# First FF1 unit with plain block products for half of the tokens, output weights parted anew, end reordered

## The chip, the cores and the metric

The kernel runs on one core of one Trainium2 chip. The metric is device time in microseconds of one execution, as the median of several runs.

## The reference

One step of a small decoder trunk over 1024 prompt tokens and 64 sample tokens (8 sequences of 8), model width 1024, all in float32:

```python
h = rmsnorm(x, g1)
z = h @ w_in                                   # 1024 x 2816, split among three mixers
ya = gelu(za_u) * spatial(layernorm(gelu(za_v)))      # A: gMLP in chunks of 128 tokens
yb = silu(layernorm(conv31(zb_a * sigmoid(zb_g))))    # B: Conformer convolution
yc = zc_b * conv3(zc_c * zc_x)                        # C: short gated convolution
x = x + concat(ya, yb, yc) @ w_out             # 1024 x 1024
x = x + square(relu(rmsnorm(x, g2) @ w_ff1)) @ w_ff2  # 1024 x 4096, 4096 x 1024
y = rmsnorm(x, gf)
```

Beside y the kernel returns the convolutions' new states and the normalised v rows.

## The kernel before

Activations are kept transposed: features on the partitions, the 1088 tokens along the free axis. Every float32 operand is parted into a high and a low part of type float32r, and a product is made of three matmuls, high x high, high x low, low x high (`mm3`, lines 170 to 176). A weight's parting takes ScalarE one copy for the high part and VectorE one subtraction for the low part (`split`, L167 and L168), or, in the input projection, ScalarE the negative of the raw weight and GpSimd a transfer that adds the weight from DRAM to it (`split_far`, L482 and L483). Weights come raw, 512 KB each, on SP's queue (`load`, L161).

The stages follow one another: the mixers' input projection (weights 0 to 17), the output projection (weights 18 to 25, one for each block `fo` of 128 output features), 16 units of FF1 and 16 of FF2, and the last RMSNorm. From the output projection on, the tokens stand in two groups, A and B, of 544 each, a group in two halves of 272.

*Output projection.* Group A goes first, while the last mixer outputs are made. Three weights are begun with `out_first` (six of eight K tiles) and ended later, five follow in `out_job`; one weight's two parts lie in `wo2`, the others in a ring of two buffers per part (`hi`, `lo`). `in_job` calls `ahead_of` at its third column block, so that weight 19 is parted by `split_far` before weight 18 is used. `out_keep` (L921) stores the parts of weights `fo` 0 to 5 to DRAM (`wod`), and `out_fetch` (L926) reads them back for group B, whose jobs run in the order 6, 7, 0, 1, 2, 3, 4, 5, each followed by one entry of the list `rest` and three of the list `todo`, which holds group A's operands for FF1. Each job ends with `out_evac`: VectorE adds PSUM to the residual (L823), ScalarE squares it (L825), VectorE sums the squares (L829).

*FF1.* A unit is a 256 x 1024 slice of w_ff1, taken as a 2 x 2 block product with the Strassen-Winograd scheme: seven products (`s` = 0 to 6) of weight sums (`w_sums`, `w_parts`, L941 to L952) with sums of the normalised tokens (`x_norm` L878, `x_hi` L884, `x_lo` L888, `x_comb` L891). `steps` (L1260) lists all products; unit 0 takes group A's seven and then group B's seven, each step 12 matmuls of 272 columns, since group B's operands are made meanwhile by the entries of `x_ops(1)`; the units 1 to 29 take both groups in one step. Unit 0's results are copied from PSUM by ScalarE (L1113) and combined, squared and split later, from the list `later`, at fixed steps of unit 0 and 1 (L1114 to L1143); the parts go to DRAM for FF2 (`gr`, `gd`). Unit 1's weights were made early and stored to DRAM (`w1d`); each is loaded when unit 0 has used that slot for the last time (L1284).

*FF2 and the end.* FF2 uses the same scheme over pairs of units; each product of a step is added by VectorE to the accumulators (`ff2_out`, L1257). The two last units, 30 and 31, take group A through both units and then group B. `beside` holds what is issued with a step, between its matmuls and its evictions: loads, weight preparation (`prep`), the split of FF2's operands (`g_split`, L1216 and L1217), and for the last norm `fin_sqs`: squares on ScalarE (L1315), their sum on VectorE (L1317), the scaling by the norm's weight on ScalarE (L1321). Group A's outputs are scaled by GpSimd during group B's steps (`fin_out`, L1329). After the last step the squares of the last two accumulators' second halves are summed by VectorE, TensorE sums over the partitions, a Newton step on VectorE (`rstd_newton`, L134 to L139) gives the factor, and VectorE scales the eight blocks of group B, each stored by SP's or ScalarE's queue.

## Time and profile before

| | |
|---|---|
| median of 3 runs | 1120.68 us (1118.84 to 1123.88) |
| the profiled execution | 1121.21 us |
| its span | 1119.5 us |
| TensorE busy | 1048.1 us (94%) |
| VectorE busy | 879.0 us (79%) |
| ScalarE busy | 418.4 us (37%) |
| mean granted TensorE clock | 0.971 |

TensorE's busy time hardly leaves room, so the profile is read by stage: where a stretch is longer than TensorE's busy time in it, or where the granted clock is under 1.00. The stages in the trace: input projection 93 to 254 us, output projection to 373.8, FF1 unit 0 to 412.3, unit 1 to 437.3, then about 21.5 us a unit, the last two units 1040.4 to 1100.3, and the rest to 1119.5.

### The profile page before, as it was taken

The numbers are of one execution on the slowest core, as the hardware profiler recorded it, in microseconds if no ns is written. First come the engines' busy times: TensorE is split into PE (matmuls) and PEld (weight loads), VectorE is DVE, ScalarE is ACT, GpSimd is POOL, SyncE is SP. The second block draws the span as 40 slices with busy tenths as digits, with TensorE's granted clock in tenths as the row PEclk, the third lists the DMA queues.
The fourth block names the chain that finished last, engine by engine and source line by source line (L and its number), as shares of the span: only waits on it lengthen the run. The fifth ranks groups of instructions, "written<-read, shape, count | busy, mean of one in ns | idle before, by whom it ended". The sixth has DMA issues, their size and how long they took to land.

```text
span 1119.5 us, 19297 instructions
## 1 busy us (share of the span) xinstructions
PE 1048.1 (94%) x7524; PEld 1021.6 (91%) x7524; DVE 879.0 (79%) x1352; ACT 418.4 (37%) x711; POOL 123.5 (11%) x161
## 2 busy tenths in 40 slices
PE   8999999997899789999999999989999999999783
PEld 6789999996889679999999999989999999999773
DVE  6886999964468788778778878886788888888775
ACT  5533455323333333434434344344322222223332
POOL 3751524212000000000000000000000000000030
PEclk8999999998999999999999999999999999999896
DMA  6213454357897355546645645698866766655012
GB/s 222 99 41 73 102 93 80 77 109 209 275 324 238 113 168 184 204 158 215 217 159 194 219 169 181 213 394 289 247 208 216 238 187 227 217 181 194 1 60 101
DMA packets 94219, 198.61 MB, mean 177 GB/s; under 512 B 18288, under 2 KB 24432, under 8 KB 94128
## 3 DMA queue, kind: packets, MB, share of 16 engines
q1 hardware_dynamic: 90240, 183.95, 48.2%
q0 software_dynamic: 3312, 12.32, 6.8%
q8 instruction: 59, 0.97, 0.4%
q10 hardware_dynamic: 576, 1.11, 0.3%
q14 instruction: 32, 0.26, 0.1%
HBM read 129.03 MB, written 68.32 MB: 176 GB/s over the span
## 4 chain that ended last, share of the span: by engine, by line
DVE 38%; PE 35%; DMA 9%; issue 8%; ACT 8%; POOL 1%; SPq 1%; ACTq 0%; DVEq 0%; POOLq 0%
PE pp L174 11%; PE pp L176 11%; PE pp L175 11%; DVE gbuf L571 3%; DVE acc L571 3%; DMA wlo<-in_w 2%; ACT wsh L951 2%; DMA gr<-x_cn 2%; DVE x_cn L1119 1%; DMA gr<-x_cm 1%; DVE x_cn L1118 1%; DVE x_cn L1127 1%; DVE x_cm L1119 1%; DVE x_cm L1118 1%; DVE x_cm L1127 1%
## 5 line engine op out<-in xcount | busy, mean ns | idle before, releaser
L176 PE MATMUL mm<-xh,wlo 128*128 128x384 f32 (+1 forms) x336 | 109.8, 327 | 1.0 <-DMA wlo<-in_w 1.0
L174 PE MATMUL mm<-xh,whi 128*128 128x384 f32 (+1 forms) x336 | 110.2, 328 | 0.0
L175 PE MATMUL mm<-xl,whi 128*128 128x384 f32 (+1 forms) x336 | 109.5, 326 | 0.0
L174 PE MATMUL pp<-xah,wsh 128*128 128x272 f32 x256 | 76.2, 298 | 5.5 <-ACT x_cm L1113 5.0
L176 PE MATMUL pp<-xah,wsh 128*128 128x272 f32 x256 | 74.5, 291 | 0.0
L175 PE MATMUL pp<-xal,wsh 128*128 128x272 f32 x256 | 74.3, 290 | 0.0
L1257 DVE TENSOR_TENSOR x_cn<-pp,x_cn 128x544 f32<-128x544 f32 (+1 forms) x100 | 61.9, 649 | 10.6 <-PE pp L176 10.5
L176 PEld LDWEIGHTS mm<-xh,wlo 128*128 128x128 f32 x336 | 63.1, 188 | 1.6 <-DMA wlo<-in_w 1.6
L174 PE MATMUL pp<-xah,wsl 128*128 128x272 f32 x208 | 61.2, 294 | 2.6 <-ACT x_cm L1113 1.8
L174 PEld LDWEIGHTS mm<-xh,whi 128*128 128x128 f32 x336 | 63.1, 188 | 0.3
L175 PEld LDWEIGHTS mm<-xl,whi 128*128 128x128 f32 x336 | 63.1, 188 | 0.3
L176 PE MATMUL pp<-xah,wsl 128*128 128x272 f32 x208 | 61.1, 294 | 0.0
L175 PE MATMUL pp<-xal,wsl 128*128 128x272 f32 x208 | 60.9, 293 | 0.0
L1257 DVE TENSOR_TENSOR acc_al<-pp,acc_al 128x544 f32<-128x544 f32 (+1 forms) x68 | 44.3, 652 | 20.1 <-PE pp L176 20.0
L1302 POOL DMA_DIRECT2D acc_ah<-x2d x2 | 1.8, 906 | 504.3 <-DMA xbl<-gd 484.1
L174 PEld LDWEIGHTS pp<-xah,wsh 128*128 128x128 f32 x256 | 48.6, 190 | 9.1 <-ACT x_cm L1113 7.1
L951 ACT ACTIVATE wsh<-x_cm 128x512 fp32r<-128x512 f32 x29 | 18.3, 632 | 82.7 <-DVE x_cm L942 82.6
L175 PEld LDWEIGHTS pp<-xal,wsh 128*128 128x128 f32 x256 | 48.8, 191 | 0.0
L176 PEld LDWEIGHTS pp<-xah,wsh 128*128 128x128 f32 x256 | 48.7, 190 | 0.0
L1257 DVE TENSOR_TENSOR acc_ah<-pp,acc_ah 128x544 f32<-128x544 f32 (+1 forms) x68 | 44.2, 650 | 2.7 <-PE pp L176 2.5
L174 PEld LDWEIGHTS pp<-xah,wsl 128*128 128x128 f32 x208 | 40.1, 193 | 3.1 <-ACT x_cm L1113 2.0
L174 PE MATMUL pp<-xbh,wsl 128*128 128x272 f32 x144 | 41.9, 291 | 0.0
(510 smaller groups left out, 3884.4 us busy)
## 6 DMA issues: line engine op xcount, KB each, us to landing
gr<-x_cn SPq DMA_DIRECT2D x64, 272.0 KB, 4.0
wraw<-in_w SPq DMA_DIRECT2D x32, 512.0 KB, 5.0
gr<-x_cm SPq DMA_DIRECT2D x56, 272.0 KB, 5.5
raw<-in_w SPq DMA_DIRECT2D x25, 512.0 KB, 6.8
wlo<-in_w POOLq DMA_DIRECT2D x15, 512.0 KB, 7.4
wrawoh<-in_w SPq DMA_DIRECT2D x15, 512.0 KB, 4.4
wrawol<-in_w SPq DMA_DIRECT2D x15, 512.0 KB, 5.8
xah<-gr SPq DMA_DIRECT2D x26, 272.0 KB, 5.6
```

The costliest lines, as they stand in the source:

```text
L174: pe.matmul(ps, ah, bh, start=first, stop=False, skip_group_check=chain)
L175: pe.matmul(ps, ah, bl, start=False, stop=False, skip_group_check=chain)
L176: pe.matmul(ps, al, bh, start=False, stop=last, skip_group_check=chain)
L571: dve.scalar_tensor_tensor(out=d, in0=src, scalar=w, in1=d, op0=ALU.mult, op1=ALU.add)
L951: act.activation(out=hi, in_=src, func=AF.Copy)
L1118: dve.tensor_tensor(out=c, in0=c if u == 0 else ps, in1=slot(add, last)[1], op=ALU.add)
L1119: dve.scalar_tensor_tensor(out=c, in0=c, scalar=0.0, in1=c, op0=ALU.max, op1=ALU.mult)
L1127: dve.tensor_tensor(out=c.bitcast(F32R), in0=c, in1=slot(name + "h", True)[1], op=ALU.subtract)
L1257: dve.tensor_tensor(out=a, in0=ps, in1=a, op=ALU.add)
L1302: at(first_use[u + 2 * i, 0] + 1, lambda fo=fos[i]: gp.dma_start(out=acc(fo), in_=x2d[fo], accum_op=ALU.add))
```

## The change

1. `in_job` no longer calls `ahead_of` for job 18, so weight 19 is parted by `split` with VectorE, when the first output job is issued, and weight 21's load comes later on SP's queue.
2. `wod`, `out_keep` and `out_fetch` go. Only the weights 6 and 7 are kept for group B; the others are loaded raw again (`out_load`) and parted anew with an accumulating transfer (`out_parts`). Group B's order is 6, 7, 3, 0, 1, 2, 4, 5.
3. In FF1 unit 0, group B takes eight plain block products (`PL`) instead of seven Strassen products; one block of the weight (`a21`) is loaded and parted anew for it. `copy` applies ReLU, `own_square` squares later. The sums of group B's tokens, which units 1 to 15 need, are made beside these steps (`beside_b`). The `later` entries move from the steps 14 to 18 to the steps 16 to 20, the load of unit 2's weights to `a21_parts`.
4. The end: unit 31's weight preparation has other steps, one split comes a step later, group B's steps of units 30 and 31 run s = 0, 1, 2, 4, 6 of both and then 3, 5 of both, with other PSUM banks for one chain. Squares of the last norm are summed behind the step's evictions (`then`). The first 256 tokens of group B are normalised and stored during the last steps (`early`); the tail treats the last 288, and TensorE sums the last squares.

```diff
-                if c == 2:
+                if c == 2 and nxt[0] < 18:
...
+    def out_load(fo):
+        wor[fo] = ring.tile([P, 1024], F32, tag="raw", name=nm("wor"))
+        sp.dma_start(out=wor[fo], in_=w[18 + fo])
+
+    def out_parts(fo, tags=("hi", "lo")):
         wob[fo] = [ring.tile([P, 1024], F32R, tag=t, name=nm("wob")) for t in tags] if tags else wo2
-        for i in range(2):
-            sp.dma_start(out=f(wob[fo][i]), in_=wod[fo, i])
+        hi, lo = wob[fo]
+        raw = wor.pop(fo)
+        act.activation(out=lo, in_=raw, func=AF.Copy, scale=-1.0)
+        gp.dma_start(out=lo, in_=w[18 + fo], accum_op=ALU.add)
+        act.activation(out=hi, in_=raw, func=AF.Copy)
...
-            if fo == 4:
-                out_fetch(3)
             if fo in (5, 6):
                 x2_fill(6 - fo, 1)
+            if fo == 5:
+                out_load(3)
             if fo == 6:
-                out_fetch(0, ("raw", "raw"))
+                out_parts(3, None)
+                out_load(0)
+            if fo == 7:
+                out_load(1)
...
+    PLAIN = 10
+    PL = [(0, 0, "c", True), (1, 1, "c", False), (2, 0, "d", True), (6, 1, "d", False),
+          (0, 6, "b", True), (2, 6, "a", True), (1, 5, "b", False), (6, 5, "a", False)]
...
+        if s >= PLAIN:
+            name = {1: "g11", 3: "g21", 6: "g12", 7: "g22"}.get(s - PLAIN)
+            if name:
+                copy(name, AF.Relu)
+            if name == "g22":
+                later.extend([lambda: (own_square("g11"), part_hi("g11", 0)), lambda: own_square("g12"),
+                              lambda: (own_square("g22"), part_hi("g22", 5)), combine, fourth] + los)
...
-            i = (2 * (u % 2) + TAGS[name] + q) % 4
+
+            i = q if g0 and name == "b" else (2 * (u % 2) + TAGS[name] + q) % 4
...
-    steps = [(0, s, (0,)) for s in range(7)] + [(0, s, (1,)) for s in (0, 1, 3, 5, 2, 4, 6)]
+    steps = [(0, s, (0,)) for s in range(7)] + [(0, PLAIN + j, (1,)) for j in range(8)]
     steps += [(u, s, (0, 1)) for u in range(1, UNITS - 2) for s in range(7)]
-    steps += [(u, s, (g,)) for g in range(2) for u in (UNITS - 2, UNITS - 1) for s in range(7)]
+    steps += [(u, s, (0,)) for u in (UNITS - 2, UNITS - 1) for s in range(7)]
+    steps += [(u, s, (1,)) for u in (UNITS - 2, UNITS - 1) for s in (0, 1, 2, 4, 6)]
+    steps += [(u, s, (1,)) for u in (UNITS - 2, UNITS - 1) for s in (3, 5)]
...
-                i = max(last_use[UNITS - 3, (2, 2, 3, 3, 4, 4, 5)[s]] + 1, first_use[u, s] - 10)
+                i = max(last_use[UNITS - 3, (2, 2, 3, 3, 4, 4, 5)[s]] + 1, first_use[u, 0] + (-10, -9, -8, -4, -3, -2, -1)[s])
...
-            at(i0 + (5, 6, 8, 9, 11, 12, 14)[s], lambda b=b, s=s: g_split(b, s))
+            at(i0 + (5, 6, 8, 9, 11, 12, 14 if b < 7 else 15)[s], lambda b=b, s=s: g_split(b, s))
...
+    def fin_sqs(i, g, fos, cut=(0, G2), half=None):
+        def sums():
+            for fo, sc in zip(fos, scs):
+                fin_add(g, fo, sc, cut)
+            if half:
+                fin_half(g, half)
+        scs = []
+        at(i, lambda: scs.extend(fin_sq(g, fo, cut) for fo in fos))
+        at(i, lambda: [fin_scale(g, fo, cut) for fo in fos])
+        then(i, sums)
...
+    for i, fos in [(-8, (0, 1)), (-7, (4, 5)), (-1, (2, 3)), (0, (6, 7))]:
+        fin_sqs(E[0] + i, 0, fos, half=(0, G2) if i == 0 else None)
+    for i, fos, t in [(2, (0, 1), 0), (5, (4, 5), 0), (7, (2, 3), 0), (10, (6, 7), 0), (11, (4, 5), 1), (12, (0, 1), 1)]:
+        fin_sqs(E[0] + i, 1, fos, TH[t])
...
+    def early():
+        ps = pair(2)
+        t = (G2, CUT[0][1])
+        sc = fin[0][:, t[0]:t[0] + t[1]]
+        stat_tok(ps, [sc], mean1k_f)
+        def pow_():
+            dve.transpose(out=sc, in_=ps[:, :t[1]])
+            rstd_pow(t, sc)
+        def outs():
+            rstd_bcast(t, sc)
+            for i, fo in enumerate((2, 0, 1, 4, 3, 6, 5, 7)):
+                fin_out(1, fo, gp if i % 2 == 0 or i > 5 else dve, sp, CUT[0])
+        then(E[0] + 11, pow_)
+        then(E[0] + 13, outs)
+    at(E[0] + 11, early)
+    last_sq = {}
+    at(E[0] + 13, lambda: last_sq.update({fo: fin_sq(1, fo, TH[1]) for fo in (6, 7)}))
+    at(E[0] + 13, lambda: [fin_scale(1, fo, TH[1]) for fo in (6, 7)])
...
-            lambda: out_fetch(4, ("hi", "lo")), lambda: out_fetch(5, ("hi", "lo")), lambda: None, slot_ring]
+    rest = [lambda: (out_parts(0), out_load(2)),
+            lambda: (out_parts(1), out_load(4)),
+            lambda: (out_parts(2, None), out_load(5)),
+            lambda: out_parts(4),
+            lambda: (out_parts(5), raw_first()),
+            lambda: None, slot_ring]
     stemp[0] = vv[0][:, 0:512]
     norm_half(0)
-    for i, fo in enumerate((6, 7, 0, 1, 2, 3, 4)):
+    for i, fo in enumerate((6, 7, 3, 0, 1, 2, 4)):
...
-    todo.extend(x_ops(1))
     prep(0, 4)
+    B11, B21, B12, B22 = (0, 0), (1, 0), (0, 1), (1, 1)
+    a21 = wraw[0][1][:, :512]
+    sp.dma_start(out=a21, in_=w[27, :, 0:512])
+    def a21_parts():
+        hi, lo = wslot[2][:, :512], wslot[2][:, 512:]
+        act.activation(out=hi, in_=a21, func=AF.Copy)
+        dve.tensor_tensor(out=lo, in0=a21, in1=f(hi), op=ALU.subtract)
+        unit_load(2)
+    def stat_last():
+        stat_rest(1, st, rb2, OC[1])
+        stemp[0] = x2_slot(7)[:, :512]
+        unit_load(3)
+    beside_b = {
+        0: lambda: (prep(0, 5), prep(0, 6), stat_mm(npart[1, OC[1]], st, OC[1])),
+        1: lambda: x_norm(1, range(4), 0),
+        2: lambda: (hi_of(1, B11, 0), x_norm(1, range(4, 8), 0)),
+        3: lambda: (hi_of(1, B21, 1), lo_of_(1, B11, 0)),
+        4: lambda: lo_of_(1, B21, 1),
+        5: stat_last,
+        6: lambda: (x_norm(1, range(4), 1), a21_parts()),
+        7: lambda: (hi_of(1, B12, 6), lo_of_(1, B12, 6)),
+        8: lambda: x_norm(1, range(4, 8), 1),
+        9: lambda: (hi_of(1, B22, 5), lo_of_(1, B22, 5)),
+        10: lambda: (x_comb(1, B11, B12, B11), hi_of(1, B11, 3)),
+        11: lambda: (x_comb(1, B12, B22, B12), hi_of(1, B12, 4), lo_of_(1, B11, 3)),
+        12: lambda: (x_comb(1, B22, B22, B11), hi_of(1, B22, 2)),
+        13: lambda: lo_of_(1, B22, 2),
+        14: lambda: (x_comb(1, B21, B21, B22), hi_of(1, B21, 6), lo_of_(1, B12, 4), lo_of_(1, B21, 6)),
+    }
     for i in range(len(steps)):
-        for _ in range({14: 5, 15: 4, 16: 3, 17: 3, 18: 3}.get(i, 0)):
+        for _ in range({16: 5, 17: 4, 18: 3, 19: 3, 20: 3}.get(i, 0)):
...
-    fin_sqs(1, (6, 7), (0, H))
-    ps = pair(0)
-    stat_mm([fin[0][:, gs(1)]], ps, (0, G2), mean1k_f)
-    stat_rest(1, ps, fin[0], (0, G2))
-    for i, fo in enumerate((0, 1, 4, 5, 2, 3, 6, 7)):
-        fin_out(1, fo, dve, act if i % 2 else sp)
+        if i in beside_b:
+            beside_b[i]()
+    ps = pair(3)
+    o = G2 + CUT[1][0]
+    stat_tok(ps, [fin[0][:, o:o + 288]], mean1k_f, last=False)
+    for fo in (6, 7, 2, 3):
+        sq = last_sq[fo] if fo in last_sq else fin_sq(1, fo, TH[1])
+        stat_tok(ps, [sq], mean1k_f, 16, False, fo == 3)
+    stat_chain(1, ps, CUT[1])
+    for fo in (2, 3):
+        fin_scale(1, fo, TH[1])
+    for i, fo in enumerate((0, 1, 4, 5, 6, 7, 2, 3)):
+        fin_out(1, fo, dve, act if i % 2 else sp, CUT[1])
```

## Rows read from the trace of the kernel before

**Rows 1.** The head of the page: the span, and each engine's busy time with its share of the span and its number of instructions.

```profile
span 1119.5 us, 19297 instructions
...
PE 1048.1 (94%) x7524; PEld 1021.6 (91%) x7524; DVE 879.0 (79%) x1352; ACT 418.4 (37%) x711; POOL 123.5 (11%) x161
```

**Rows 2.** The table by stage: the window, its length, then the busy time (and instructions) of TensorE, TensorE's weight loads, VectorE, ScalarE and GpSimd, the granted TensorE clock, the share of time that the 16 transfer engines were busy, and GB/s. The windows are, in order: output projection of group A after its first weight; output projection of group B; FF1 unit 0; unit 1; group A in units 30 and 31; group B in units 30 and 31; the rest.

```profile
260.20:324.70 64.50, 51.87 (x352) 49.85 (x351) 29.52 (x45) 17.99 (x29) 4.82 (x4) 0.87 0.85 289
324.70:373.80 49.10, 49.10 (x390) 48.94 (x388) 38.91 (x59) 18.05 (x24) 0.00 (x0) 1.00 0.68 233
376.50:412.30 35.80, 25.39 (x173) 23.51 (x174) 30.84 (x58) 14.32 (x27) 0.00 (x0) 0.95 0.43 139
412.30:437.30 25.00, 23.21 (x171) 22.79 (x170) 18.20 (x37) 9.07 (x19) 0.00 (x0) 0.93 0.55 183
1040.40:1070.50 30.10, 24.49 (x170) 23.89 (x169) 22.14 (x44) 10.77 (x18) 0.00 (x0) 0.89 0.01 1
1070.50:1100.30 29.80, 24.36 (x174) 23.28 (x172) 20.73 (x44) 11.18 (x19) 12.02 (x8) 0.94 0.19 75
1100.30:1119.50 19.20, 2.16 (x5) 1.18 (x4) 10.66 (x22) 4.26 (x11) 0.00 (x0) 0.56 0.32 117
```

**Rows 3.** The list of waits between 254 and 325 us (group A's output projection): engine and line, what it waited for, us in total, number of times, the longest.

```profile
ACT whi L167 <- DMA wod<-whi: 11.4, 3, 4.8
...
DVE wlo L168 <- DMA wod<-wlo: 8.3, 2, 5.2
...
PE pp L176 <- DMA wlo<-in_w: 7.2, 1, 7.2
...
PE pp L176 <- DVE wlo L168: 3.3, 4, 1.0
...
PE pp L174 <- ACT whi L167: 2.2, 3, 1.2
```

**Rows 4.** The same kind of table for stretches at a low granted clock (columns as in rows 2).

```profile
268.10:273.20 5.10, 5.10 (x22) 5.10 (x23) 1.03 (x2) 0.62 (x2) 0.00 (x0) 0.50 1.03 417
300.50:303.90 3.40, 3.40 (x16) 3.40 (x15) 1.93 (x3) 1.70 (x3) 0.00 (x0) 0.50 0.89 248
310.70:314.10 3.40, 3.40 (x17) 3.40 (x16) 2.36 (x4) 0.91 (x2) 0.00 (x0) 0.50 0.98 364
...
1048.00:1054.80 6.80, 5.80 (x26) 5.83 (x26) 4.93 (x11) 0.73 (x2) 0.00 (x0) 0.50 0.01 2
```

**Rows 5.** The timeline of four engines around weight 19's wait (start, duration, engine, line, operation; in brackets the idle time before it and what ended it): ScalarE's and VectorE's parting into `wo2`, TensorE's first product after the wait, SP's loads into `x_cm` and of weight 21.

```profile
258.87 1.04 ACT L167 ACTIVATE wo2h<-raw 128x1024 fp32r<-128x1024 f32 x1
...
259.94 1.23 DVE L168 TENSOR_TENSOR wo2l<-raw,wo2h 128x1024 fp32r<-128x1024 f32 x1 [1.46 <-ACT acc L747]
...
268.07 0.61 PE L176 MATMUL pp<-yah,wlo 128*128 128x288 f32 x1 [7.21 <-DMA wlo<-in_w]
...
262.22 2.63 SPq L796 DMA_DIRECT2D x_cm<-in_x  x4
...
265.96 0.48 SPq L161 DMA_DIRECT2D raw<-in_w  x1
```

**Rows 6.** Transfers with accumulation: the page's list of DMA issues (count, KB each, median us from issue to landing), the last line of the view of tile `wlo` (shortest, median and longest time to landing), and a window inside the input projection (columns as in rows 2).

```profile
wlo<-in_w POOLq DMA_DIRECT2D x15, 512.0 KB, 7.4
...
DMA to landing us min/median/max: 6.2/7.5/13.0
...
160.00:220.00 60.00, 60.00 (x366) 60.00 (x365) 58.94 (x77) 25.41 (x61) 18.80 (x37) 1.00 0.42 89
```

**Rows 7.** The steps of a chain in group B's output projection: VectorE's eviction of a job and ScalarE's square of it, from the timeline, and the view of tile `wlo` for ScalarE's low part (count, shortest, median and longest ns, first and last start).

```profile
345.70 0.71 DVE L823 TENSOR_TENSOR x_cm<-pp,x_cm 128x544 f32<-128x544 f32 x1
...
346.83 0.64 ACT L825 ACTIVATE vv<-x_cm 128x544 f32<-128x544 f32 x1
...
L482 ACT ACTIVATE wlo<-raw x15: 1043/1052/1062, 78.6 to 253.6; 128x1024 fp32r<-128x1024 f32 x15
```

**Rows 8.** The timeline of FF1 units 0 and 1: two first products of TensorE's steps, one of each unit, with the wait ahead of them, a low part of group B's operand and the first 272-column operation on unit 0's results on VectorE, and a weight part there; and from the list of DMA issues between 385 and 436 us the load of one of unit 1's weights (columns as in rows 6).

```profile
397.37 0.39 PE L174 MATMUL pp<-xah,wsv 128*128 128x272 f32 x1 [3.07 <-ACT x_cm L1113]
...
429.62 0.39 PE L174 MATMUL pp<-xah,wsl 128*128 128x272 f32 x1 [1.79 <-ACT x_cm L1113]
...
407.27 1.29 DVE L888 TENSOR_TENSOR xbl<-x_cn,xbh 128x1088 fp32r<-128x1088 f32 x1
408.48 0.43 DVE L1118 TENSOR_TENSOR x_cm<-x_cm 128x272 f32<-128x272 f32 x1
...
416.76 0.69 DVE L952 TENSOR_TENSOR wo2h<-wraw,wo2h 128x512 fp32r<-128x512 f32 x1 [2.02 <-ACT wo2h L951]
...
wo2h<-w1d SPq DMA_DIRECT2D x1, 512.0 KB, 4.4
```

**Rows 9.** The timeline of the end: TensorE's wait in group A's units and its statistics product after the last product, VectorE's split of a g operand, the first of the output scalings, and the last transfer's issue.

```profile
1049.00 0.56 PE L174 MATMUL pp<-xb_yl,wsh 128*128 128x272 f32 x1 [3.42 <-DVE acc_ah L1257]
...
1104.58 1.73 PE L842 MATMUL pp<-fin,means 128*128 128x288 f32 x3 [4.27 <-DVE fin L1317]
...
1047.21 1.29 DVE L1217 TENSOR_TENSOR xbl<-xbl,xbh 128x1088 fp32r<-128x1088 f32 x1 [0.31 <-ACT xbh L1216]
...
1109.83 0.73 DVE L1329 TENSOR_TENSOR acc_ah<-acc_ah,fin 128x544 f32<-128x544 f32 x1
...
1115.08 0.34 ACTq L1330 DMA_DIRECT2D out_y<-x_cn  x1
```

103 lines of the change are left out of this document (51 added, 52 removed).

## The prediction

> **What bounds the kernel now.** I read the head of the page first [rows 1]: TensorE is busy for 94% of the span, so time can only leave where TensorE idles, runs at half clock, or where work follows its last product. Then the table by stage [rows 2], to find those places. The reader is to compare the length of each stretch with TensorE's busy time and with the granted clock. Five stretches matter. Output projection of group A, 64.5 us: 12.6 idle, clock 0.87. Output projection of group B, 49.1 us: no idle, clock 1.00. FF1 unit 0, 35.8 us: 10.4 idle, with VectorE busy for 30.8 of it. The end of group A in the last two units, 30.1 us: 5.6 idle, clock 0.89. The tail after the last product, 19.2 us. Units 1 to 29 are TensorE-bound apart from the first, and the change leaves all of them but units 1 and 2 alone. Last, the list of waits of the first stretch [rows 3] says who ends the idle time there.
>
> The profiled execution took 1121.21 us: the span of 1119.5 [rows 1] and 1.7 around it. The sums are made against it; the median of the three runs, 1120.68, lies 0.5 below and I take that off at the end. About 0.5% (5.6 us) is what a measurement of this kernel can tell from no change.
>
> **Group A's output projection.** Three things hold TensorE [rows 3]: 7.2 us for the accumulating transfer of weight 19's low part, 3.3 for VectorE's low parts and 2.2 for ScalarE's high parts of later weights. The last two are late because the buffers of these parts are still being stored to `wod` (11.4 us of ScalarE's and 8.3 of VectorE's waiting). After each wait the clock is at half [rows 4]: 5.1 + 3.4 + 3.4 = 11.9 us of busy time at 0.50, so 5.95 us lost. Idle and clock together: 12.6 + 5.95 = 18.6 us.
> The change removes the transfer (weight 19 is parted by ScalarE and VectorE) and the stores. What is late next: the new parting takes the place in both queues that the parting into `wo2` has [rows 5], high part at 258.9 to 259.9 and low part 1.2 us long, done about 260.3 to 261.2; TensorE wanted the low part at 260.70 (its third product, before the 7.21 us wait). So 0 to 0.5 us of wait is left, and one of the four waits on VectorE's low parts, at weight 22, before any store is in the way, stays (under 1.0) [rows 3]. Weight 21's load is moved on SP's queue past the four loads into `x_cm`, which issue from 262.22 to 264.9, so it issues at about 265 and not ahead of them; in the trace it stands at 265.96 anyway [rows 5], behind two stores that go away. It costs nothing unless TensorE, now 7 us earlier, reaches it first: up to 1 us, and one more half-clock stretch if so. I take -18. Bounds: -18.6 (nothing left) and -13 (one wait of 3 us and a clock stretch left).
>
> **Group B's output projection.** Six weights were fetched in two parts by SP; now each is loaded raw and parted by ScalarE (low = -raw, then high) and by an accumulating transfer that GpSimd issues. ScalarE gains 12 operations of 1.05 us, 12.6 us, beside 18.1 busy of 49.1 [rows 2, 7]: room enough, though each stands ahead of that job's squares. The traffic stays about as it was (six weights, two transfers each). The chain of one buffer pair: its job (6.1 us: 49.1 over eight jobs), then the eviction 0.71, the square about 1.1 behind it, the low part 1.05, with queueing and the issue some 4.5 us in all [rows 7], then the landing, median 7.4 us over 15 such transfers [rows 6]. Three pairs rotate, so a job can start every (6.1 + 4.5 + 7.4)/3 = 6.0 us: just under the job's own 6.1. With no slack, delays show: about half a microsecond for five of six weights, +2.5 us. Bounds: 0, and 13.0 us each, the longest landing in the trace [rows 6]: (6.1 + 4.5 + 13.0)/3 - 6.1 = 1.8 us for each of six, +11. I lean to the median, because it lies 1.3 us above the shortest landing and 5.5 below the longest; the longest is that of weight 19 (its landing ended the 7.21 us wait), in group A's stretch, where the transfer engines are at 0.85; group B's stretch has 0.68 [rows 2], and in the 60 us at 0.42 [rows 6] TensorE was busy throughout, so none came too late there.
> The Trainium skill, "DMA: Bandwidth & Descriptors", section "Anatomy of one DMA — SWDGE (gpsimd) path", fits 2.0 us + bytes/436e3; for 512 KB that would be 3.2 us, an estimate, and group B would then wait for nothing. The trace disagrees: 7.4 us at the median [rows 6].
>
> **FF1 unit 0 and unit 1.** Group B's seven Strassen products become eight plain ones: one step more, 12 products of 272 columns, 1.5 us of TensorE. The plain ones need only normalised quarters and their splits, so they no longer wait for chains of sums. VectorE: four additions and squares of 0.43 us are saved [rows 8], one low part of 1.29 and one weight part of 0.69 added, near zero in all. VectorE's total for unit 0 and the operations that follow therefore stays, 30.8 + 18.2 us of busy time in 60.8 [rows 2], but TensorE waits less in unit 0. Of its 10.4 us of idle time the largest parts are PSUM copies that stand on ScalarE's queue behind group B's high parts (3.07 us in one place [rows 8]), and group B's operands come later than the products could; both go, since the copies of the plain products and the operands alternate. With 1.8 us more from the clock (0.05 of 35.8) and 1.5 less for the step more, at most 10.7 us; a replay in order of issue leaves some waits for copies and ends group B's products 9 us earlier, at 403 on the old scale. Unit 1 then needs group B's sums (slots 3, 4, 2, 6), which VectorE finishes about 411 on that scale, and after them the squares and splits of unit 0's results. So TensorE waits in unit 1 where it didn't: about 0.8, 3.2, 1.3 and 2.9 us at four of its steps, against one wait of 1.79 and one half-clock stretch before. Unit 1's own weights, loaded when a slot has had its last use in unit 0, now have three to four steps of 1.5 us for a landing of 4.4 [rows 8] where they had up to seven: no slack, 0 to 0.5 us of it on the path, inside the bounds. Unit 2 starts 4 us earlier, not 9. I take -4. Bounds: -8 (VectorE keeps up) and 0 (TensorE's waits in unit 1, with a half-clock stretch of 1.7 us lost behind each of the two long ones, eat all of it).
> The Trainium skill, "TensorE: Matmul & The Clock Gate", section "HAM oscillation — how this bites in real kernels", says that gaps in TensorE's work bring the clock down and that what follows starts slow. By it this edit would lose what it gains, through the two long waits (a term of 0, rival 3); the trace agrees behind the waits of 7.21 and 3.42 us [rows 4, 5, 9].
>
> **The end.** In group A's last units TensorE waits 3.42 us for evictions that stand behind the weight sums and the 1.29 us split on VectorE [rows 9], and the stretch 1048.0 to 1054.8 runs at half [rows 4]: 5.8 busy, 2.9 lost. The change spreads the preparation and puts the split a step later: of 6.3 us I take 5, because the sums still stand close to the evictions; the other 2.2 us of idle time in the stretch [rows 2] stay. In group B the squares' sums go behind the evictions, but steps are also reordered, and the statistics of group A still stand on VectorE between two evictions that TensorE needs; I take no change of the 29.8 us.
> The tail: from the last product to the end 19.2 us [rows 2]. From the statistics product to the first output scaling 5.25 us [rows 9], 544 wide; at 288 wide the product halves (1.73 to 0.9) and two transposes halve (as long as a 544-column operation, 0.73, each: -0.7): 3.7. Eight scalings of 288 columns at about 0.43, as the 272-column operation [rows 8], follow: 3.4, where 5.2 stand now (from 1109.83 to the last issue at 1115.08). From the last issue to the end 4.4, unchanged. Ahead of all this the eviction (0.43) and two squares (half of 0.64 [rows 7] each) with their way to TensorE: 1.2 in place of 4.27, since VectorE no longer adds the last squares. 1.2 + 3.7 + 3.4 + 4.4 = 12.7: -6.5. The early outputs of 256 tokens go to GpSimd and VectorE in the last steps, where VectorE has 9 us free of 29.8. Together -11.5; bounds -5 (tail alone, partly) and -14.
>
> **The sum.** -18 + 2.5 - 4 - 11.5 = -31: 1121.2 - 31 = 1090.2, by the median of the runs 1089.7, so 1090.
>
> **The rivals.**
> 1. The accumulating transfers land late beside group B's load (13 us each): +11 in place of +2.5, 1098. For it: the landing of 13.0 in a busy stretch, and no slack in the rotation [rows 6]. Against it: the median. Chance 0.15.
> 2. The transfers land so late that the kernel is slower. One mechanism: GpSimd is held off between the issue and the landing while VectorE works, and group B's stretch has VectorE busy for 38.9 of 49.1 us [rows 2]. It decides from where six waits eat 33.5 us, 5.6 each: (6.1 + 4.5 + L)/3 = 11.7, L = 24.5 us; at 28 us each the time is 1121.2 - 33.5 + 6 x 6.8 = 1128. Against it: between 160 and 220 us VectorE was busy for 58.9 of 60 us, and TensorE, which these transfers feed there, for all 60 [rows 6]. Chance 0.04. The Trainium skill, "SBUF — State Buffer", section "SBUF: two separate sides", warns of it for VectorE's two-port modes; the trace doesn't show it.
> 3. VectorE eats the whole gain of unit 0 in unit 1: 0 in place of -4, 1094. Chance 0.15.
> 4. The end gives only its tail, 1095 to 1097, since the reordered steps make new waits. Chance 0.1.
> 5. The change does not do what it says, because another wait ends where weight 19's did (weight 21's raw, the `wo2` parts): -5 in place of -18, 1103. Chance 0.06. Within it, with group B's transfers late as well, the gain nearly vanishes: 1115 to 1121, chance 0.04, the case of no change.
>
> **How the numbers follow.** My forecast, all terms near their values, has 0.46, and gives 1090. Rivals 1, 3, 4 and 5 are all faster. Range: the low end takes group A, unit 0 and the end near their best, -18.6 - 6 - 13 with 0 in group B: 1083, rounded to 1081 for a unit 0 at its bound; the high end takes rival 1 with a unit 0 at 0: 1102, rounded to 1104 to hold rival 5 too. Outside: below 0.08, above 0.12. Faster by over 0.5%: 0.92; within: 0.04; slower: 0.04.
>
> **What would show it.** Right: no TensorE wait on an accumulating transfer near 260; clock 1.00 through group A's projection, which ends about 18 us earlier; waits under 1 us at the starts of group B's jobs; unit 0's products about 9 us shorter with new waits in unit 1 on copies and group B's slots; the tail near 12.7 us. Wrong: transfers of 10 us and more in group B's projection; unit 2 starting as long after group B's projection as before; a half-clock stretch in the last 60 us at the old place.

## The result, and the profile after

The changed kernel takes 1092.87 us (median of 4 runs, 1092.58 to 1094.44), the kernel before, run beside it, 1122.28. The ratio is 0.9742, with a 95% interval of 0.971 to 0.9774. The prediction was 1090, with a range of 1081 to 1104.

The head of the page of the changed kernel answers to [rows 1]: the span is 28.7 us shorter, and TensorE's busy time only 7.4.

```profile
span 1090.8 us, 19364 instructions
...
PE 1040.7 (95%) x7544; PEld 1016.7 (93%) x7544; DVE 879.3 (81%) x1357; ACT 432.0 (40%) x733; POOL 132.7 (12%) x173
```

So about 21 us of the gain are waits and tail. The other 7.4 us are TensorE's own busy time, mostly because less of the work runs at half clock (the mean granted clock is 0.982 for 0.971). The table by stage answers to [rows 2]. Its windows: output projection of group A after its first weight, group B's, FF1 unit 0, units 1 and 2, then group A in units 30 and 31, group B there, and the rest.

```profile
259.40:305.20 45.80, 44.87 (x352) 44.16 (x351) 29.83 (x46) 17.70 (x29) 4.82 (x4) 1.00 0.71 236
305.20:357.20 52.00, 49.53 (x390) 49.07 (x388) 39.39 (x60) 29.32 (x36) 5.23 (x6) 1.00 0.85 243
360.50:385.90 25.40, 24.68 (x183) 24.21 (x183) 21.66 (x43) 12.35 (x23) 0.00 (x0) 0.95 0.56 191
385.90:416.90 31.00, 24.44 (x171) 23.81 (x170) 25.50 (x46) 12.37 (x23) 0.00 (x0) 0.89 0.46 161
416.90:439.40 22.50, 21.39 (x170) 21.16 (x169) 18.16 (x28) 8.55 (x15) 0.00 (x0) 1.00 0.55 184
1023.50:1047.40 23.90, 21.91 (x171) 21.32 (x170) 20.72 (x43) 10.71 (x18) 0.00 (x0) 1.00 0.01 2
1047.40:1078.60 31.20, 25.53 (x177) 24.55 (x176) 23.08 (x51) 15.54 (x36) 13.04 (x10) 0.89 0.19 72
1078.60:1090.80 12.20, 2.44 (x10) 1.67 (x10) 8.29 (x21) 2.01 (x6) 3.99 (x5) 0.69 0.57 183
```

The reader is to compare again the length with TensorE's busy time. Group A's projection has lost nearly all its idle time and runs at 1.00. Unit 0 has 0.7 us of idle time where it had 10.4. Unit 1 has 6.6 where it had 1.8, at 0.89. Group A's last units have 2.0 at 1.00, group B's 5.7 at 0.89.

From the first product of each stage to that of the next, in the profiled executions before and after, and as predicted:

| stage | before | after | change | predicted |
|---|---|---|---|---|
| output projection, group A | 70.0 | 51.3 | -18.7 | -18 |
| output projection, group B | 48.9 | 51.9 | +3.1 | +2.5 |
| unit 0 | 35.0 | 25.4 | -9.6 | -9 |
| units 1 and 2 | 46.4 | 53.5 | +7.2 | +5 |
| units 3 to 15 | 279.4 | 279.5 | +0.1 | 0 |
| unit 16, the first of FF2 | 27.6 | 29.7 | +2.1 | 0 |
| units 17 to 29 | 274.8 | 274.8 | 0.0 | 0 |
| units 30 and 31, group A | 30.1 | 23.9 | -6.2 | -5 |
| units 30 and 31, group B | 29.8 | 31.2 | +1.4 | 0 |
| after the last product | 19.2 | 12.3 | -6.9 | -6.5 |

(What is missing to 28.7 lies in the input projection, 0.8, and ahead of unit 0, 0.4.) Lengths of stages that wait are not exact: group A's projection takes 70.0 us in the kernel before, and 68.2 and 70.1 in two of the kernels below that don't touch it; group B in units 30 and 31 takes 29.8, and 28.3 in one; unit 16 27.6, and 28.4 to 28.6 in four that leave unit 0 as it was. So a difference of 1 to 2 us in one stage of one profile is read with care.

TensorE's timeline of the changed kernel has these waits among others: one in group A's projection, two in group B's, the two long ones in unit 1, one at the start of FF2, and the longest of group B's last steps.

```profile
280.82 0.40 PE L176 MATMUL pp<-yah,wlo 128*128 128x288 f32 x1 [0.68 <-DVE wlo L168]
...
326.42 0.40 PE L176 MATMUL pp<-yah,wob 128*128 128x288 f32 x1 [2.02 <-DMA wob<-in_w]
...
351.38 0.40 PE L176 MATMUL pp<-yah,wob 128*128 128x288 f32 x1 [0.45 <-DMA wob<-in_w]
...
394.76 0.39 PE L174 MATMUL pp<-xah,wsh 128*128 128x272 f32 x1 [2.00 <-ACT x_cn L1131]
...
405.22 0.59 PE L174 MATMUL pp<-xah,wsh 128*128 128x272 f32 x1 [4.15 <-ACT x_cm L1131]
...
726.76 0.59 PE L174 MATMUL pp<-xb_yh,wo2h 128*128 128x272 f32 x1 [6.13 <-ACT x_cn L1131]
...
1057.71 0.59 PE L174 MATMUL pp<-xb_yl,wsh 128*128 128x272 f32 x1 [3.39 <-DVE acc_ah L1280]
```

Each row names in brackets how long TensorE stood and what came last. The row at 280.82 is the one wait that was to stay in group A's projection. In unit 1 both waits are for ScalarE's copies of a product out of PSUM. ScalarE's own timeline says why these copies were late:

```profile
394.08 0.62 ACT L1131 ACTIVATE x_cn<-pp 128x544 f32<-128x544 f32 x1 [1.42 <-DVE xbl L917]
...
404.55 0.62 ACT L1131 ACTIVATE x_cm<-pp 128x544 f32<-128x544 f32 x1 [2.85 <-DMA gr<-x_cm]
```

The first copy stood until VectorE's last low part of group B's operand had read the place into which it goes. The second waited 2.85 us for a transfer to store what its place in the staging buffer held. So both copies wait for places, and VectorE stands behind both places: its timeline has one gap, of 1.18 us, from 382.8 to 404.9 us. The low part that the first copy waits for (392.70 to 393.99) lies in this stretch. So does, by the order in which the code issues them, the low part (from 400.40) whose store the second waits for.

### The profile page after: what moved, and what is told of

Read it like the earlier page. It is cut to its first block, busy times and chain, and to the rows that moved or that the text cites. A ratio compares the mean times of both kernels' runs of the same rounds, so it can differ in the third digit from the quotient of the medians.

```text
span 1090.8 us, 19364 instructions
## 1 busy us (share of the span) xinstructions
PE 1040.7 (95%) x7544; PEld 1016.7 (93%) x7544; DVE 879.3 (81%) x1357; ACT 432.0 (40%) x733; POOL 132.7 (12%) x173
## 4 chain that ended last, share of the span: by engine, by line
PE 30%; DVE 18%; issue 6%; ACT 5%; DMA 3%; ACTq 0%; DVEq 0%
PE pp L174 10%; PE pp L176 10%; PE pp L175 10%; ACT wsh L962 2%; DMA gr<-x_cn 2%; DVE x_cn L1137 1%; DVE x_cm L1137 1%; DVE x_cn L1136 1%; DVE x_cn L1145 1%; DVE x_cm L1136 1%; DVE x_cm L1145 1%; DMA gr<-x_cm 1%; DVE x_cm L953 1%; DVE x_cm L1149 1%; ACT wsl L962 1%
## 5 line engine op out<-in xcount | busy, mean ns | idle before, releaser
L174 PEld LDWEIGHTS pp<-xah,wsh 128*128 128x128 f32 x256 | 48.6, 190 | 11.5 <-ACT x_cm L1131 5.9
L176 PE MATMUL pp<-xbh,wsl 128*128 128x272 f32 x140 | 40.5, 289 | 0.0
L174 PE MATMUL pp<-xbh,wsl 128*128 128x272 f32 x140 | 40.4, 288 | 0.0
```

The lines of the kernel that those rows point to most:

```text
L174: pe.matmul(ps, ah, bh, start=first, stop=False, skip_group_check=chain)
L176: pe.matmul(ps, al, bh, start=False, stop=last, skip_group_check=chain)
```

## The experiments

Four kernels make one part of the change alone, from the kernel before. **Part 1**, weight 19:

```diff
-                if c == 2:
+                if c == 2 and nxt[0] < 18:
```

> The kernel before with the first part of the change alone (weight 19 parted by ScalarE and VectorE). Theory, the two kinds of wait are separate: the 7.2 us wait on the accumulating transfer and the 2.5 us of its half-clock stretch go, the rest of group A's projection stays, so about 9.7 us less, 1112. Rival, the stores to DRAM set the pace of the later weights: TensorE comes to them earlier and waits longer there, so the gain is 3 to 6 us and the waits on VectorE's and ScalarE's parts grow from 5.5 us by about what the first wait loses.

1112.22 us against 1119.06, ratio 0.9936 (0.9912 to 0.9961). Group A's projection is 8.0 us shorter. Its list of waits, the answer to [rows 3]:

```profile
DVE wlo L168 <- DMA wod<-wlo: 14.4, 3, 5.9
...
ACT whi L167 <- DMA wod<-whi: 13.0, 3, 5.4
...
PE pp L174 <- ACT whi L167: 5.3, 3, 2.6
...
PE pp L176 <- DVE wlo L168: 3.4, 4, 1.0
```

The wait on the transfer is gone, but TensorE's waits on the parts have grown from 5.5 to 8.7 us, and ScalarE's and VectorE's waits on the stores from 19.7 to 27.4. The rival had the mechanism in part: the waits on the parts grow by 3.2 us, where it wanted about the 7.2 that the first wait lost. The gain, 6.8 us, lies between the two figures.

**Part 2**, weights parted anew in place of stored and read back:

```diff
             if fo == 6:
-                out_fetch(0, ("raw", "raw"))
+                out_parts(3, None)
+                out_load(0)
...
+        gp.dma_start(out=lo, in_=w[18 + fo], accum_op=ALU.add)
```

> The kernel before with the second part alone (no stores of the parts, group B's weights loaded raw and parted anew). Theory: the waits on parts held by stores (5.5 us less one of 0.7 that no store causes) and the two half-clock stretches behind them (3.4 us) go from group A, and group B's projection, which had no wait, gets about 2.5 to 3 us of waits: 5 to 6 us less in all, 1116, with the 7.2 us wait on weight 19 still there. Rival, the accumulating transfers land late beside group B's traffic: landings over 10 us and a net of 0 or worse.

1112.55 us, ratio 0.9937 (0.9916 to 0.9959), 6.5 us less than the kernel before. Group A's projection is 11.4 us shorter, group B's 3.7 longer. TensorE's waits in group A's projection:

```profile
PE pp L176 <- DMA wlo<-in_w: 5.2, 1, 5.2
...
PE pp L176 <- DVE wlo L168: 0.9, 2, 0.7
```

All that the stores caused is gone. The wait on weight 19 is shorter as well, 5.2 for 7.2, with less half clock behind it, so group A gains 11.4 us and not the 8.2 of the expectation's terms. The six accumulating transfers of group B land after 5.7 to 9.1 us, so the rival falls. Parts 1 and 2 together take 18.7 us from group A's projection; alone they take 8.0 and 11.4, so they add to within 0.7 us.

**Part 3**, unit 0's plain products:

```diff
-    steps = [(0, s, (0,)) for s in range(7)] + [(0, s, (1,)) for s in (0, 1, 3, 5, 2, 4, 6)]
+    steps = [(0, s, (0,)) for s in range(7)] + [(0, PLAIN + j, (1,)) for j in range(8)]
```

> The kernel before with the third part alone (unit 0's plain products for group B). Theory, what unit 0 gains is given back in unit 1: unit 0 shorter by 9 to 10 us, units 1 and 2 longer by 6 to 7, net 2 to 4 us less, 1119. Rival, the give-back in the changed kernel comes from the other parts (an earlier group B, other transfers): then this part alone keeps 8 us or more, 1113.

1118.26 us, ratio 0.9994 (0.9975 to 1.0012): no difference. The table by stage, unit 0, unit 1, unit 2 and unit 16:

```profile
376.90:404.30 27.40, 26.88 (x184) 26.39 (x183) 22.05 (x43) 12.50 (x23) 0.00 (x0) 0.84 0.52 180
404.30:433.30 29.00, 23.47 (x171) 22.84 (x170) 25.22 (x46) 12.09 (x23) 0.00 (x0) 0.94 0.48 166
433.30:456.80 23.50, 21.71 (x171) 21.27 (x170) 18.21 (x28) 8.55 (x15) 0.00 (x0) 1.00 0.54 181
736.10:765.10 29.00, 23.01 (x171) 22.79 (x170) 24.12 (x33) 14.21 (x22) 0.94 (x1) 0.88 1.04 384
```

Unit 0 is 7.6 us shorter than before, at a granted clock of 0.84 (the changed kernel has 0.95 there, and 25.4 us). Unit 1 is 4.0 us longer, unit 2 2.1 and unit 16 1.4, so 0.1 is left at the start of unit 17. It is the change's own doing, as the theory had it, and more of it than expected.

**Part 4**, the end:

```diff
+    steps += [(u, s, (1,)) for u in (UNITS - 2, UNITS - 1) for s in (0, 1, 2, 4, 6)]
+    steps += [(u, s, (1,)) for u in (UNITS - 2, UNITS - 1) for s in (3, 5)]
```

> The kernel before with the fourth part alone (the end reordered). Theory: group A's last units lose the 3.4 us wait and its half-clock stretch, 5 to 6 us; group B's stay or grow by 1 to 2; the tail loses 6.5 to 7: 11 to 12 us less in all, 1110. Rival, the end's gain hangs on how the last units are reached (transfers and weights of units before): then 8 us or less.

1109.34 us, ratio 0.9907 (0.9878 to 0.9937). Group A in the last units, group B, the rest:

```profile
1040.60:1064.50 23.90, 21.92 (x170) 21.32 (x169) 20.69 (x43) 10.68 (x18) 0.00 (x0) 1.00 0.01 2
1064.50:1095.80 31.30, 25.64 (x177) 24.65 (x176) 23.12 (x51) 15.61 (x36) 13.04 (x10) 0.89 0.19 72
1095.80:1107.96 12.16, 2.41 (x10) 1.64 (x10) 8.25 (x21) 1.97 (x6) 3.99 (x5) 0.69 0.57 183
```

23.9, 31.2 and 12.2 us, as in the changed kernel to 0.1 us. The end stands by itself, and with 9.7 us less the rival (8 or less) falls.

By the spans of the profiles the four parts alone give 10.1, 7.6, 0.6 and 11.5 us, 29.8 together, and the whole change 28.7. By the times their four ratios multiply to 0.9776, and the whole change has 0.9742 (0.971 to 0.9774). So nothing here shows a gain that needs two parts at once.

The other kernels start from the changed one. **Without part 3:**

```diff
-    steps = [(0, s, (0,)) for s in range(7)] + [(0, PLAIN + j, (1,)) for j in range(8)]
+    steps = [(0, s, (0,)) for s in range(7)] + [(0, s, (1,)) for s in (0, 1, 3, 5, 2, 4, 6)]
```

> The changed kernel with unit 0's part undone (parts 1, 2 and 4 kept). Theory, the plain products pay next to nothing because units 1 and 2 give the time back: 0 to 3 us above the changed kernel, ratio to the kernel before 0.974 to 0.977. Rival, in the changed kernel they keep the 4 us of the prediction or more: ratio 0.978 to 0.982.

1094.73 us, ratio 0.9758 (0.9742 to 0.9774); the changed kernel has 0.9742 (0.971 to 0.9774). The profiled spans lie 3.0 us apart (1093.9 and 1090.8). Of the stages that part 3 acts on, unit 0 gives 10.4, units 1 and 2 take back 7.2, and unit 16 takes back 1.3 (it takes 28.4 us here), so 1.9 are left; the other 1.1 lie in stages that part 3 leaves alone. The theory's figures came true and the rival's did not. The intervals overlap, so part 3 is worth 2 to 3 us by the traces and cannot be told from nothing by the times.

**Two copies of unit 1 into another buffer:**

```diff
+                if key in ((1, "p0"), (1, "u2")):
+                    stn[0] += 1
+                    j = G2 if name == "u2" else 0
+                    stg[key] = rb2[:, j:j + G2]
```

> The changed kernel; in unit 1 two staging copies (of products 0 and 2) go into the buffer of the row factors, free by then, in place of two slots in the normalised tokens' tile. Theory, slots: unit 1's waits of 2.0 and 4.15 us are ScalarE's copies that wait for a slot (for VectorE's last split that reads it, for a transfer that stores it), so both waits go and unit 1 takes 24 to 26 us in place of 31.0, with 1 to 3 us of new waits behind. Rival, VectorE's amount of work (25.5 us busy of 31.0): the waits move to the next steps and units 1 and 2 together keep 52 us or more of the 53.5.

1093.99 us (one run). TensorE's waits in unit 1:

```profile
393.91 0.39 PE L174 MATMUL pp<-xah,wsh 128*128 128x272 f32 x1 [0.38 <-ACT rb L1136]
...
402.99 0.39 PE L174 MATMUL pp<-xah,wsh 128*128 128x272 f32 x1 [2.77 <-ACT rb L1136]
...
407.28 0.39 PE L174 MATMUL pp<-xah,wsl 128*128 128x272 f32 x1 [1.00 <-ACT x_cm L1136]
```

The first wait fell from 2.00 to 0.38, the second from 4.15 to 2.77: that much of the two waits, 1.6 and 1.4 us, was for the places. The rest of the second copy's lateness is ScalarE's queue ahead of it. Unit 1 takes 28.5 us, more than the theory's 24 to 26. A third wait appears there, and in unit 2 VectorE's square waits 4.05 us for the store of a place:

```profile
DVE x_cn L1141 <- DMA gr<-x_cn: 4.1, 1, 4.1
```

Units 1 and 2 take 54.7 us together, 1.2 more than before this edit. The rival's figure came true, by another way than its own: not VectorE's work but the next place's store.

**Leftover work of unit 0 spread evenly, with the same two copies moved and their places free for others:**

```diff
-        for _ in range({16: 5, 17: 4, 18: 3, 19: 3, 20: 3}.get(i, 0)):
+        for _ in range({16: 2, 17: 4, 18: 4, 19: 4, 20: 4}.get(i, 0)):
```

> The changed kernel with the two staging copies of unit 1 in the row factors' buffer (as in the run before with that buffer, but their slots stay free for others) and unit 0's leftover work spread evenly over the steps 16 to 20 (2, 4, 4, 4, 4 entries in place of 5, 4, 3, 3, 3). Theory, VectorE's order: its leftover work stands ahead of unit 1's first square, on which ScalarE's queue and the copies wait; with less of it in front, units 1 and 2 take 50 to 52 us in place of 53.5. Rival, VectorE's amount: 52.5 us or more, with the waits at later steps.

1091.76 us (one run). Units 1, 2 and 16:

```profile
386.60:416.40 29.80, 23.79 (x170) 22.72 (x169) 27.18 (x49) 12.38 (x23) 0.00 (x0) 0.94 0.46 163
416.40:437.60 21.20, 21.20 (x171) 21.20 (x170) 16.88 (x26) 8.45 (x15) 0.00 (x0) 1.00 0.58 198
716.60:747.80 31.20, 23.64 (x169) 23.19 (x169) 23.29 (x33) 14.30 (x22) 0.86 (x1) 0.89 1.02 375
```

Units 1 and 2 take 51.0 us, 2.5 less, with VectorE's busy time in unit 1 higher (27.2 us) than ever. Unit 2 has no wait left. Unit 16 takes 31.2 in place of 29.7, so 0.8 us is left at the end. The edit moves both the order of the leftover work and the places, so the 2.5 us are not parted between these two.

**Without unit 0's low parts:**

```diff
-            dve.tensor_tensor(out=c.bitcast(F32R), in0=c, in1=slot(name + "h", True)[1], op=ALU.subtract)
+            if u:
+                dve.tensor_tensor(out=c.bitcast(F32R), in0=c, in1=slot(name + "h", True)[1], op=ALU.subtract)
+            else:
+                slot(name + "h", True)
```

> The changed kernel without unit 0's eight low-part subtractions (left out: the low parts that unit 0 hands to FF2 are the values themselves, so y is not the reference's; stores and copies stay). It takes 3.4 us of VectorE's work out of units 1 and 2. Theory, VectorE's amount sets these units: they take 3 to 4.5 us less than the 53.5. Rival, slots and stores set them: under 1.5 us less.

1092.14 us (one run). Units 1 and 2:

```profile
386.70:416.40 29.70, 24.89 (x170) 24.32 (x169) 22.48 (x38) 12.07 (x23) 0.00 (x0) 0.89 0.48 164
416.40:439.40 23.00, 21.66 (x170) 21.22 (x169) 18.15 (x28) 8.55 (x15) 0.00 (x0) 1.00 0.53 181
```

VectorE has 3.0 us less to do in unit 1, and the two units take 52.8 us, 0.8 less; unit 0 takes 26.8 in place of 25.4, as it does in two kernels below that leave it alone. Both copies wait as long as before, 1.42 and 2.83 us for 1.42 and 2.85. The theory that VectorE's amount of work sets these units falls: 3.0 us of it gave 0.8. That the order of VectorE's work and the places do is what the two runs before point to.

**FF2's first two splits behind unit 15's sums:**

```diff
-        at(i + 4, lambda s=s: g_split(0, s))
+        (then if s in (1, 2) else at)(i + 4, lambda s=s: g_split(0, s))
```

> The changed kernel; two splits of FF2's first operands are issued behind unit 15's last sums and not ahead of them. Theory, the queue: at the start of FF2 TensorE waits 6.1 us (4.8 before) for ScalarE's last copy of unit 15, which stands behind VectorE's sums, which stand behind a split that waits for its load to land; with the splits behind, the wait is under 1.5 us and unit 16 takes 22 to 24 us in place of 29.7. Rival, the loads' landing itself sets the end (the second product of unit 16 needs the split): the wait moves there and unit 16 keeps 28 us or more.

1089.60 us (one run). TensorE's wait is 3.16 in place of 6.13 us, and unit 16 takes 27.5 in place of 29.7. Neither figure was met: the queue was half of it.

**Group B's low parts by VectorE:**

```diff
-        act.activation(out=lo, in_=raw, func=AF.Copy, scale=-1.0)
-        gp.dma_start(out=lo, in_=w[18 + fo], accum_op=ALU.add)
         act.activation(out=hi, in_=raw, func=AF.Copy)
+        dve.tensor_tensor(out=lo, in0=raw, in1=f(hi), op=ALU.subtract)
```

> The changed kernel with group B's low parts made by VectorE (a subtraction of 1.23 us) in place of ScalarE's negative and the accumulating transfer. Theory, the 2.0 us wait there comes from the raw weight landing late (9 us behind four loads), the transfers' landings of 5.5 to 8.7 us only add to it: group B's projection 50 to 51 us in place of 51.9. Rival, VectorE with 39.4 us busy of 52 has no room: its queue delays the parts or the evictions, 52 us or more, and unit 0 later starts no earlier.

1100.21 us (one run), 7.7 us more in the trace. Group B's projection and the time from its last job to unit 0:

```profile
304.80:359.70 54.90, 51.46 (x390) 50.61 (x388) 42.14 (x59) 22.15 (x27) 0.00 (x0) 0.97 0.46 169
359.70:368.20 8.50, 1.12 (x4) 0.71 (x4) 6.39 (x12) 2.67 (x6) 0.00 (x0) 0.74 0.14 50
```

The projection takes 54.9 us, and unit 0 starts 8.5 us after its last job's second half and not 3.3. The rival holds, though VectorE is idle for 12.8 of the 54.9 us: its queue runs late even so, and TensorE waits 7.4 us behind it, for the operand of the norm's sums, before unit 0. The accumulating transfer is what buys VectorE's time for group A's operands.

**Three edits in three stages:** weights 3 and 0 loaded ahead of other loads; at FF2's start the splits one step further back and the last copy ahead of the weight parts; the last norm's factor of group A behind that step's evictions.

```diff
-            if fo in (5, 6):
-                x2_fill(6 - fo, 1)
             if fo == 5:
                 out_load(3)
...
                 out_parts(3, None)
                 out_load(0)
+            if fo in (5, 6):
+                x2_fill(6 - fo, 1)
...
-        at(i + 4, lambda s=s: g_split(0, s))
+        (then if s in (1, 2) else at)(i + 4 + (s == 1), lambda s=s: g_split(0, s))
...
+        if (u, s) == (15, 6):
+            ff1_out(u, s, gr)
         for job_ in beside.pop(i, []):
...
+    then(E[0] + 2, lambda: stat_rest(0, sps[0], fin[0], (0, G2)))
```

> The changed kernel with three edits in three stages. (1) Weights 3 and 0 are loaded raw ahead of the loads into x_cn and x_cm: if the 2.0 us wait in group B's projection comes from weight 0's raw landing late, it goes and the projection takes 50 us in place of 51.9; if it comes from the accumulating transfer itself (7.6 us to land), under 1 us is won. (2) At FF2's start the splits go one step further back and unit 15's last copy ahead of that step's weight parts: with the queue as the cause the wait, 6.1 us and 3.2 with the first edit of this place, falls under 2 us and unit 16 takes 25 to 26.5 us; if the first operands' landing sets it, it stays at 27.5 or more. (3) The factor of group A's last norm is worked out behind that step's evictions: with VectorE's order as the cause the 3.4 us wait in group B's last steps goes and these take 28 to 29.5 us in place of 31.2; if the accumulation chain sets it, the wait moves by one step and under 1 us is won.

1090.16 us (one run). TensorE's waits in the three stages:

```profile
325.89 0.40 PE L176 MATMUL pp<-yah,wob 128*128 128x288 f32 x1 [1.80 <-DMA wob<-in_w]
...
721.91 0.39 PE L174 MATMUL pp<-xb_yh,wo2h 128*128 128x272 f32 x1 [1.65 <-ACT x_cn L1131]
...
725.88 0.39 PE L175 MATMUL pp<-xb_yh,wo2l 128*128 128x272 f32 x1 [2.05 <-DVE xb_yh L1239]
...
1057.32 0.39 PE L174 MATMUL pp<-xbh,wsv 128*128 128x272 f32 x1 [2.13 <-DVE x_cn L1280]
...
1067.66 0.39 PE L174 MATMUL pp<-xbh,xbh 128*128 128x272 f32 x1 [1.84 <-DVE x_cn L1280]
```

(1) The wait is 1.80 for 2.02; the projection is 1.0 us shorter and unit 0 1.3 longer. Kernels that leave this place alone lie between 0.9 us under and 1.0 over the changed one there, so nothing is won that can be told from chance. The raw weight's landing was a small part of the cause: ScalarE's low part starts 1.4 us earlier, now behind the first job's square, and then the accumulating transfer takes 8.5 us in place of 7.6. (2) The copy's wait falls to 1.65, and a new one of 2.05 for the split of FF2's operand takes its place; unit 16 keeps 29.2, as the rival had it. (3) The wait of 3.39 becomes 2.13 and a later one grows from 0.74 to 1.84; group B's last steps take 29.6 us in place of 31.2, because no half-clock stretch follows (1.00 there, 0.89 in the changed kernel).

**The edits that won, together** (spread leftover work, the splits behind unit 15's sums, the factor behind the evictions):

> The changed kernel with the edits that won time in single looks: unit 1's two copies in the row factors' buffer with the leftover work spread evenly (units 1 and 2: 51.0 in place of 53.5), FF2's two first splits behind unit 15's sums (unit 16: 27.5 in place of 29.7 to 31.2), group A's last factor behind the evictions (group B's last steps: 29.6 in place of 31.2). Theory, the three are in separate stages and add: 6.2 us less than the changed kernel, a span of 1084 to 1085, 1086 us and a ratio of 0.969 to the kernel before. Rival, a wait moved from one stage comes back in another (units 1 and 2's stores and FF2's first loads go through the same queue): 3 us or less, a ratio of 0.9715 or more.

1092.60 us (5 runs, 1090.93 to 1093.17), ratio 0.9762 (0.9741 to 0.9782): no better than the changed kernel. Units 1 and 2 give 2.7 us; unit 16 takes 33.0, 3.3 more; group B's last steps 31.2, nothing won. Those two stages:

```profile
716.00:749.00 33.00, 24.99 (x170) 24.32 (x170) 22.89 (x32) 14.31 (x22) 0.86 (x1) 0.90 1.02 362
1047.70:1078.80 31.10, 25.07 (x177) 23.82 (x175) 23.83 (x51) 15.49 (x36) 12.84 (x10) 0.95 0.19 73
```

The rival's figure came true. In the second stage the half-clock stretch is back, 0.95 in place of 1.00, with nearly the same waits. In the first, ScalarE's eviction into `x_cn`, where four of FF2's accumulators lie, waits for a store of FF1's last results, and TensorE waits behind it:

```profile
740.62 1.14 ACT L1282 ACTIVATE x_cn<-pp 128x544 f32<-128x544 f32 x2 [5.82 <-DMA gr<-x_cn]
...
741.30 0.40 PE L174 MATMUL pp<-xb_yl,wsl 128*128 128x272 f32 x1 [3.42 <-ACT x_cn L1282]
```

The run with the spread leftover work alone has the same two waits, 5.38 and 1.34 us. In the changed kernel, in the one with the splits moved alone, and in the first one with unit 1's two copies in the other buffer, the eviction waits 1.1 to 1.3 us.

The code says where the difference comes from. The staging places are taken in turn, 13 a unit out of 15 (`ST`). The first run with the other buffer counted the two moved copies (`stn[0] += 1`). The two later edits don't, so every later copy stands two places back in the turn. Unit 15's last copy shows it: TensorE waits for it in `x_cm` here and in `x_cn` in the kernel with the splits moved alone.

```profile
720.78 0.40 PE L174 MATMUL pp<-xb_yh,wo2h 128*128 128x272 f32 x1 [3.15 <-ACT x_cm L1135]
...
723.08 0.39 PE L174 MATMUL pp<-xb_yh,wo2h 128*128 128x272 f32 x1 [3.16 <-ACT x_cn L1131]
```

By the same count, the low part that unit 15 stores last (issued at 734.46) now lies where unit 16 puts its first accumulator in `x_cn`. So the loss comes with the edit of unit 1's copies. It is not shown that reaching FF2 earlier costs anything, nor that the transfers as such set unit 16's length: their engines are at 1.02 to 1.04 there at 27.5 us as at 33.0. No run spread the leftover work with the places kept, so this cause is read from the code and the rows and is not tested.

## Why the prediction was right, by its own steps

**Group A's output projection, -18; measured -18.7.** Right in mechanism and size. The wait that was to stay (under 1.0) is there with 0.68 us, and weight 21's load costs nothing. Parts 1 and 2 alone show that the two causes add to within 0.7 us.

**Group B's output projection, +2.5; measured +3.1.** Right in size. The landings into `wob`, four of the six, are 5.5 to 7.6 us, by the last line of the view of that tile; the two into `wo2` take 8.7 and 6.9.

```profile
DMA to landing us min/median/max: 5.5/7.4/7.6
```

So rivals 1 and 2 fall, though the transfer engines are at 0.85 in this stage too, as in the one with the landing of 13.0 us. The small delays for five of six weights are not what happened: weight 0 alone has a wait of 2.02 us, where the prediction wanted all under 1, another one has 0.45, and the rest came in time. The estimate by the Trainium skill, "DMA: Bandwidth & Descriptors", section "Anatomy of one DMA — SWDGE (gpsimd) path", of 3.2 us for 512 KB stays under the landing of every one of these transfers.

**Unit 0 and unit 1, -4; measured -2.5 up to unit 3, and about -1 with unit 16.** Unit 0's -9 was right (-9.6). The term that was off in size is the give-back, +5 predicted and +7.2 measured. Its mechanism was right: VectorE finishes group B's sums and parts at 394.0, which is 411 on the old scale (unit 1 starts at 385.9 here and at 403 there), and the first wait hangs on that; the second hangs on the store of a place, and VectorE's work of unit 0 comes before that store. The four waits of 0.8 to 3.2 us, 8.2 together, became two long ones and some short ones, 7.7 us in units 1 and 2. What the sum put at nothing is the clock. It took off the old half-clock stretch and put none in its place, and had one only in its bound of 0. Measured is a stretch at half clock of 6.8 us, in which 5.6 us of products cost 2.8 more:

```profile
403.99:410.82 6.83, 5.60 (x24) 5.60 (x25) 5.14 (x12) 3.79 (x8) 0.00 (x0) 0.50 0.48 162
```

It starts inside the wait of 4.15 us; behind the wait of 2.00 us the clock stays at 1.00. So the rule of the Trainium skill, "TensorE: Matmul & The Clock Gate", section "HAM oscillation — how this bites in real kernels", by which gaps in TensorE's work bring the clock down, is borne out behind one of the two waits. Rival 3, no gain at all from this part, is what part 3 alone shows (0.9994); in the whole change the trace leaves it 1.9 us.

**The start of FF2, not in the prediction: +2.1.** It was taken as untouched, and it is the step that was left out. One wait of 6.13 us stands there, where the kernel before has 4.76:

```profile
744.46 0.60 PE L174 MATMUL pp<-xb_yh,wo2h 128*128 128x272 f32 x1 [4.76 <-ACT x_cn L1113]
```

The 1.4 us more of wait and a longer half-clock stretch behind it make the 2.1. With two splits moved the wait is 3.16 and the unit as short as in the kernel before (27.5), so half of the wait is the order of the queues. Part 3 brings 1.3 to 1.4 us of the 2.1, since that is what it adds alone and what goes when it is undone. By what way it does so is open; it also moves the staging places by one (`stn` starts at 12 and not at 13).

**The end, -11.5; measured -11.7.** Group A's wait and half-clock stretch are gone, -6.2 for -5. Group B's steps, taken as unchanged, are 1.4 longer, with a wait of 3.39 us at the place that the prediction named, the factor of group A between two evictions, and a half-clock stretch behind it. The tail is 12.3 us for 12.7, though not in the predicted shares: VectorE scales three early outputs, 2.2 us (1079.49 to 1081.64), before it turns to the last factor, so that from the last product to the first scaling it is 5.8 us and not 4.9, and the scalings and the last landing make up for it. Rival 4 falls.

The sum was -31, measured are -28.7 in the traces. The 2.3 us between them are 2.1 at the start of FF2, 1.5 in units 0 and 1, 0.6 in group B's projection, less 0.7 in group A's, 0.2 at the end and 1.1 in stages that the sum left out, to rounding. That 4.2 us one way met 2.0 the other is luck.

## What to carry to other kernels

Cost a stage to the end of what it delays: an operand or a staging place that is made later than it was is paid one or two units further on, and here 7.2 of 9.6 us came back. Price the waits that you forecast with the clock behind them: here that was 2.8 us in one unit. Where a copy waits, look at what its destination holds and who still has to read or store that, and then at what stands ahead of that reader or store. When an edit frees or moves a place in a ring, follow the ring to its end: two places less in unit 1 changed which copy lies in the way of another stage, fifteen units later.

## What the runs showed of the hardware that was not expected

- TensorE's half-clock stretches come and go with waits of nearly the same length: group B's last steps have waits of 1.5, 2.1, 0.4 and 1.8 us and run at 1.00 in one kernel (three edits), and with waits of 1.5, 2.1, 1.5 and 0.9 us at 0.95 in another (the edits that won, together), which costs 1.5 us. Each is one profile.
- A stage without waits repeats exactly: units 17 to 29 take 274.82 us in all 14 kernels. Unit 16, with the transfer engines at 1.02 to 1.04, takes 27.5 to 33.0 us with the same products, as the order in the queues and the staging places differ.
- Six subtractions of 1.23 us on VectorE in place of six accumulating transfers of 5.5 to 8.7 us made the kernel 7.7 us slower in the trace, with VectorE idle for 12.8 us of the stage's 54.9.
